# DeltaNet steps: keys and queries of a chunk side by side as one stationary operand

## The chip, the cores and the metric

The kernel runs on one core of one Trainium2 chip. The core has five engines that work at the same time: TensorE (PE) for matrix products, VectorE (DVE), ScalarE (ACT) and GpSimd (POOL) for the rest, SyncE (SP) for issuing transfers, and 16 DMA engines. Each engine runs its instructions in the order in which they were put in; semaphores make it wait for others. The metric is the time of one execution in microseconds (us), the median of several; smaller is better. A profile comes from one further execution.

## The reference

The program is a two-layer diffusion backbone over 256 latent and 256 context tokens of width 1024, in float32. Each layer is half a SwiGLU FFN, a token mixer, and half a FFN. The mixer of layer 0 is a bidirectional gated DeltaNet with 8 heads of width 128; that of layer 1 is windowed attention. The change is in the DeltaNet. Its tokens are cut into chunks of 64; within a chunk a triangular system is solved, and from chunk to chunk a 128x128 state is carried, once forwards and once backwards through the sequence:

```python
kb = k * beta[..., None]
lower = jnp.where(strict, jnp.einsum('nhcid,nhcjd->nhcij', kb, k) * decay, 0.0)
rhs = jnp.concatenate([v * beta[..., None], kb * jnp.exp(gc)[..., None]], axis=-1)
uw = lax.linalg.triangular_solve(lower, rhs, left_side=True, lower=True, unit_diagonal=True)
u, w = uw[..., :dv], uw[..., dv:]
qk = jnp.einsum('nhcid,nhcjd->nhcij', q, k) * decay
qg = q * jnp.exp(gc)[..., None]
kd = k * jnp.exp(g_last[..., None] - gc)[..., None]

def step(state, inp):
    u_c, w_c, qk_c, qg_c, kd_c, a_c = inp
    v_new = u_c - jnp.einsum('nhik,nhkv->nhiv', w_c, state)
    o = jnp.einsum('nhik,nhkv->nhiv', qg_c, state) + jnp.einsum('nhij,nhjv->nhiv', qk_c, v_new)
    state = state * a_c[..., None, None] + jnp.einsum('nhjk,nhjv->nhkv', kd_c, v_new)
    return state, o
```

In each step the state is multiplied by something made from the chunk's keys and by something made from its queries.

## The kernel before

The kernel keeps 128x512 tiles: 128 features by 512 tokens, or 128 tokens by four pieces of 128 features. The FFN and all projections are products of 128x128 weights with 128x512 activations; each float32 operand is split in a high and a low part, and three products of those make one accurate one (rows `mm<-u 128x512`). The DeltaNet's own small products (`mm<-u 128x128`, `64x128`, `64x64`) are plain float32, and the profile has two records for each of those.

**Order.** The kernel is written as tasks (Python generators) under a planner, `Sched`. The planner has a clock of its own, with a cost for each operation (a matmul's `ns`, a cost per element on the other engines). Whenever PE would have to wait for a task's operand by that clock, it steps other tasks. So the order of the instructions on all engines is fixed when the program is built, and an edit in one task moves the work of others. All matmuls are issued from one line, L280 (transposes on PE from L285), all other operations from L184; the tiles tell them apart.

**DeltaNet.** Units of projection come in the order `DN_ORDER`: keys, gate z, queries, values of heads 0 to 3 (group 0), then keys, values, queries, z of heads 4 to 7 (group 1). Each unit is convolved over the tokens (`u<-mm,cw,u`, five taps on DVE) and put through SiLU (`dn_unit`). Chunks are kept in four pairs q; a pair is a forward chunk on partitions 0 to 63 and its backward partner on 64 to 127. For each group runs `dn_group`: `dn_prep` makes the K·K products (`mm<-u 64x64`, `dn_pairs`) and their decay; `dn_solve` inverts the triangular blocks, 31 column steps of two DVE operations (`u<-big`, `big<-big,u`), then two transposes on DVE (`STREAM_TRANSPOSE big<-big`), then 32x32 products on PE (`mm<-big,ub`, `mm<-ub,u`); `dn_kq` makes the K·Q products and multiplies the decay on (`u<-mm,u` 128x512). There is one solve per group, solve 0 and solve 1. Group 1's keys, queries, values and decayed keys Ke pass through DRAM (`KTD`, `QD`, `VD`, `KD`), and are loaded when the chains of group 0 are done.

**Chains.** `dn_chain(h)` runs the eight steps (`STEPS`) of one head; four heads of a group run interleaved, chain 0 then chain 1. `dn_expand` puts the two 64x64 blocks of a pair into block-diagonal 128x128 tiles U and KQ. In each step with s≥1:

1. two matmuls with the 64 columns of a chunk's keys as stationary operand, one into each half of the partitions of `ps`, each with its direction's state S (a column pair, K);
2. DVE: r = neg·ps + Vt, one operation over 128 partitions (`u<-mm,neg,u`);
3. PE: U·r; ACT copies it as w;
4. PE: two products of a half of Ke (64 rows) with w (a Ke pair); two column-half products of the queries with S (a Q pair); KQ·w;
5. DVE: two updates of S (`u<-u,aS,mm`); ACT: a copy o and qs = eg·(Q·S) (`u<-mm,eg`); POOL adds them.

`dn_out` normalises the outputs by pairs of heads, transposes them and multiplies by the gate. The product of z with the output gain (`u<-u,ogain`) belongs to the z units, which are stored to `ZD`.

Of the kernel before, what the change touches and what calls it, by code (L numbers as in the profile page):

```python
# [213 lines left out]
class Kernel:  # L214
# [842 lines left out]
    def dn_gates(self, ps):  # L1057
# [52 lines left out]
        nc.vector.tensor_scalar(out=self.neg, in0=self.eg, scalar1=-1.0, scalar2=None, op0=ALU.mult)  # L1110
        self.kdw = self.const([128, 2, 4, 8], "kdw")
# [5 lines left out]
    def dn_unit(self, kind, h, ps):  # L1117
# [21 lines left out]
        yield self.at(acc)  # L1139
        for o, i in zip(self.pieces(t, True), self.pieces(acc, False)):  # L1140
            self.act(out=o, in_=i, func=AF.Silu)
        if kind < 2:
            (self.qT if kind == 0 else self.kT)[h] = t
        if kind == 0:
            sq = self.u()
            self.act(out=sq, in_=t, func=AF.Square)
            self.qsq[h] = sq
            return
# [25 lines left out]
    def dn_ss(self, sq, g, dst):  # L1174
# [12 lines left out]
        for i in range(4):  # L1187
            del sq[4 * g + i]

    def dn_pairs(self, ps, lhs, rhs, g, qp):  # L1190

        for q2 in range(2):
            for i in range(4):
                for half in range(2):
                    c0 = 128 * (2 * qp + q2) + 64 * half
                    o = 256 * q2 + 64 * i
                    self.mm(ps[64 * half:64 * half + 64, o:o + 64], lhs[4 * g + i][:, c0:c0 + 64],
                            rhs[4 * g + i][:, c0:c0 + 64], ns=75)

    def dn_prep(self, g):  # L1200
# [27 lines left out]
        for qp in range(2):  # L1228
            ps = self.mmt()
            self.dn_pairs(ps, self.kT, self.kT, g, qp)  # L1230
            G.append(self.u())
            self.act(out=G[qp], in_=ps, func=AF.Copy)
            yield 500
# [153 lines left out]
    def dn_expand(self, g, k):  # L1387
# [8 lines left out]
        for s, (q, e) in enumerate(self.STEPS):  # L1396
# [5 lines left out]
            else:  # L1402
                src = self.UB[g][:, x:x + 4, :]
            for hf in (slice(0, 64), slice(64, 128)):
                dst = tiles[s % nb].rearrange("p (h i) -> p h i", h=4)[hf, :, hf]
                if k and g == 0:
# [6 lines left out]
    def dn_chain(self, h):  # L1413
# [4 lines left out]
        while (h, 0) not in self.Ke or (h, 1) not in self.Ke:  # L1418
            yield 300
        kT, Vt = self.kT[h], self.Vt[h]  # L1420
        half = [slice(0, 64), slice(64, 128)]
        for s, (q, e) in enumerate(self.STEPS):
            cs = slice(128 * q, 128 * q + 128)
            c0 = [128 * q, 128 * q + 64]
            while (g, 0, s) not in self.blk:
# [42 lines left out]
            self.step[h] = s  # L1468
            yield self.at(po[:, 0:256])
            eg = self.eg[:, e, q, h:h + 1]  # L1470
            o = O[:, cs] if e == 0 else wv
            self.act(out=o, in_=po[:, 128:256], func=AF.Copy)
# [9 lines left out]
        self.chained.add(h)  # L1482
        for d in (self.kT, self.qT, self.Vt):
            del d[h]
# [10 lines left out]
    def dn_group(self, g):  # L1495
# [7 lines left out]
        if g:  # L1503
# [8 lines left out]
            for h in hs:  # L1512
                load(self.Ke, (h, 0), self.KD[2 * h - 8])
            for d, src in ((self.kT, self.KTD), (self.qT, self.QD)):
                for h in hs:
                    load(d, h, src[h - 4])
            for h in hs:
# [9 lines left out]
    def dn_out(self, p):  # L1527
# [29 lines left out]
        for h in hs:  # L1557
# [4 lines left out]
            t = self.u()  # L1562
            for o, i, z in zip(self.pieces(t, False), self.pieces(ps, True), self.pieces(zg[h], False)):
                nc.vector.tensor_tensor(out=o, in0=i, in1=z, op=ALU.mult)
            ps = None
# [27 lines left out]
    def deltanet(self, nxt):  # L1593
# [15 lines left out]
        self.KD = self.dp.tile([8, 128, 512], F32, name="KD", tag="KD")  # L1609
        self.QD = self.dp.tile([4, 128, 512], F32, name="QD", tag="QD")  # L1610
        self.KTD = self.dp.tile([4, 128, 512], F32, name="KTD", tag="KTD")
        self.VD = self.dp.tile([4, 128, 512], F32, name="VD", tag="VD")
# [291 lines left out]
```

## Time and profile before

| what | value |
|---|---|
| runs | 1927.81, 1928.87, 1933.45 us; median 1928.87 |
| profiled execution | 1928.68 us; its span 1926.9 us, granted PE clock 0.992 |
| first FFN | about 0 to 385 us |
| DeltaNet | about 385 to 800 us; solve 0 486.75 to 552.10, solve 1 606.65 to 685.70, chain 1 699.70 to 771.30 |
| two FFNs | about 800 to 1540 us |
| attention and last FFN | about 1540 to 1927 us |

How to read it: a row of the timeline or of the weight loads gives start, busy time, engine (PEld is a weight load), line, operation, the tiles (out<-in), the shape and a count of records; in brackets the idle time ahead and what ended it. A row of a table by window gives the window's length, then each engine's busy time with its count of instructions, the granted PE clock, the share of the DMA engines, and GB/s. In a row of instructions grouped by form the busy time and the mean in ns stand behind the bar, then the idle time ahead of them. The chain of waits follows the end of the program back from wait to wait. Matmul ends are modelled, and a few per cent of the records can be missing, so prices of matmuls are taken from starts.

### The profile page before, as it was taken

How to read it: one execution, taken by the hardware profiler on the slowest of the kernel's cores; microseconds unless marked ns; L12 is line 12 of the kernel's file. 1: busy time of each engine (PE TensorE's matmuls, PEld its weight loads, DVE VectorE, ACT ScalarE, POOL GpSimd, SP SyncE). 2: the span in 40 equal slices, each digit the busy share in tenths (PEclk: the TensorE clock that was granted, in tenths of full speed). 3: DMA queues.
4: the chain of work that ended last, by engine and by line, in shares of the span. 5: the costliest groups of instructions: out<-in, count | busy, mean ns of one | idle time of the engine just before them, and what ended most of it. 6: DMA issues, size and time to landing. Idle time of an engine off the chain costs nothing.

```text
span 1926.9 us, 30122 instructions
## 1 busy us (share of the span) xinstructions
PE 1868.2 (97%) x11335; PEld 1558.2 (81%) x11335; DVE 1278.8 (66%) x2097; ACT 949.4 (49%) x2062; POOL 649.3 (34%) x597
## 2 busy tenths in 40 slices
PE   7999999999999999999999999999999999899999
PEld 5878788887777766887888888888888899689999
DVE  4897878865986975478988655743333355956555
ACT  4545535457466555465455344641322248865442
POOL 3344434453545536254444124420000047230000
PEclk9999999999999999999999999999999999999999
DMA  9655554423222252444655454433223425125652
GB/s 292 209 199 202 177 186 170 141 61 115 83 68 87 66 182 83 162 156 150 208 196 195 170 190 155 153 126 109 89 90 106 132 66 110 45 67 176 197 176 88
DMA packets 242665, 271.31 MB, mean 141 GB/s; under 512 B 11047, under 2 KB 198719, under 8 KB 242519
## 3 DMA queue, kind: packets, MB, share of 16 engines
q1 hardware_dynamic: 242231, 269.21, 43.1%
q8 instruction: 89, 1.46, 0.3%
q14 instruction: 57, 0.47, 0.1%
q0 software_dynamic: 144, 0.11, 0.0%
q10 hardware_dynamic: 144, 0.07, 0.0%
HBM read 258.86 MB, written 10.49 MB: 140 GB/s over the span
## 4 chain that ended last, share of the span: by engine, by line
PE 55%; DVE 7%; ACT 3%; issue 3%; POOL 1%; DMA 1%; POOLq 0%; DVEq 0%; ACTq 0%; SPq 0%
PE mm L280 54%; DVE u L184 7%; ACT u L184 3%; PE mm L285 1%; POOL u L184 1%; DVE st L184 0%; DVE big L184 0%; DMA u<-ZD 0%; DMA u<-XD 0%; DVE ub L184 0%; ACT L184 0%; POOLq L184 0%; DVEq L184 0%; DVE sc L184 0%; ACT sc L184 0%
## 5 line engine op out<-in xcount | busy, mean ns | idle before, releaser
L280 PE MATMUL mm<-u 128*128 128x512 f32 (+5 forms) x10112 | 1784.9, 342 | 21.2 <-ACT u L184 8.2
L280 PEld LDWEIGHTS mm<-u 128*128 128x128 f32 (+2 forms) x10112 | 1490.4, 185 | 296.4 <-issue 42.0
L184 POOL TENSOR_TENSOR u<-u 128x512 f32<-128x512 f32 (+4 forms) x389 | 430.2, 1112 | 908.8 <-ACT u L184 868.9
L184 ACT ACTIVATE u<-u 128x512 fp32r<-128x512 f32 (+8 forms) x339 | 162.1, 490 | 494.0 <-DVE u L184 478.7
L184 ACT ACTIVATE u<-mm 128x128 f32<-128x128 f32 (+3 forms) x356 | 141.7, 413 | 262.4 <-PE mm L280 199.4
L184 DVE TENSOR_TENSOR u<-raw,u 128x512 fp32r<-128x512 f32 (+2 forms) x272 | 217.3, 842 | 27.7 <-ACT u L184 26.6
L184 DVE SCALAR_TENSOR_TENSOR u<-u,cc 128x512 f32<-128x512 f32 x196 | 228.2, 1164 | 4.5 <-DMA u<-in_ada_w 1.2
L184 DVE TENSOR_TENSOR u<-ub,u 128x512 fp32r<-128x512 f32 x254 | 200.3, 832 | 17.3 <-ACT u L184 15.9
L184 ACT ACTIVATE u<-raw 128x512 fp32r<-128x512 f32 (+1 forms) x374 | 205.9, 604 | 11.0 <-DMA raw<-in_ffn_w 6.6
L184 ACT ACTIVATE u<-u,cc 128x512 f32<-128x512 f32 x224 | 152.0, 711 | 83.2 <-DMA u<-in_ada_w 76.6
L184 DVE TENSOR_TENSOR u<-u,mm 128x512 f32<-128x512 f32 (+1 forms) x88 | 54.5, 620 | 206.5 <-PE mm L280 198.2
L184 POOL TENSOR_TENSOR u<-raw,u 128x512 fp32r<-128x512 f32 x98 | 130.3, 1354 | 140.2 <-ACT u L184 123.7
L184 ACT ACTIVATE u<-ub 128x512 fp32r<-128x512 f32 (+1 forms) x284 | 156.1, 605 | 9.5 <-PE mm L280 4.4
L184 DVE SCALAR_TENSOR_TENSOR u<-mm,mod,u 128x256 f32<-128x256 f32 x192 | 86.1, 477 | 108.6 <-PE mm L280 108.3
L184 DVE TENSOR_TENSOR u<-u 128x512 fp32r<-128x512 f32 (+5 forms) x125 | 84.4, 676 | 73.1 <-ACT u L184 71.6
L184 DVE SCALAR_TENSOR_TENSOR u<-u,mod 128x256 f32<-128x256 f32 (+1 forms) x140 | 89.1, 688 | 23.9 <-ACT u L184 23.6
L184 ACT ACTIVATE u<-u,mod 128x256 fp32r<-128x256 f32 (+1 forms) x124 | 56.2, 501 | 52.3 <-DVE u L184 51.6
L184 DVE SCALAR_TENSOR_TENSOR u<-mm,cw,u 128x510 f32<-128x510 f32 (+1 forms) x96 | 71.2, 743 | 8.1 <-ACT u L184 6.4
L285 PE MATMUL mm<-ident,u 128*128 128x128 f32 (+3 forms) x361 | 57.2, 291 | 15.3 <-DVE u L184 7.7
L285 PEld LDWEIGHTS mm<-ident,u 128*128 128x128 f32 (+3 forms) x361 | 43.9, 150 | 27.8 <-ACT u L184 7.5
L280 PE MATMUL mm<-u,ones 128*32 128x512 f32 (+2 forms) x172 | 38.8, 557 | 13.0 <-DVE u L184 8.9
L184 POOL TENSOR_TENSOR u<-ub,u 128x512 fp32r<-128x512 f32 x30 | 41.2, 1396 | 9.8 <-ACT u L184 9.5
(116 smaller groups left out, 567.2 us busy)
## 6 DMA issues: line engine op xcount, KB each, us to landing
u<-in_ada_w SPq DMA_DIRECT2D x256, 256.0 KB, 5.7
ub<-in_ffn_w SPq DMA_DIRECT2D x59, 1024.0 KB, 5.2
raw<-in_ffn_w SPq DMA_DIRECT2D x57, 1024.0 KB, 5.2
raw<-in_dn_w_in SPq DMA_DIRECT2D x16, 1024.0 KB, 5.7
ub<-in_ada_w SPq DMA_DIRECT2D x12, 512.0 KB, 7.3
ub<-in_ffn_w SPq DMA_DIRECT2D x8, 768.0 KB, 4.6
raw<-in_ffn_w SPq DMA_DIRECT2D x8, 768.0 KB, 4.5
raw<-in_dn_w_out SPq DMA_DIRECT2D x4, 1024.0 KB, 6.2
```

The lines of the kernel that those rows point to most:

```text
L184: r = f(*a, **k)
L280: self.nc.tensor.matmul(out, lhsT, rhs, start=start, stop=stop, **kw)
L285: self.nc.tensor.transpose(out, in_, self.ident[:k, :k])
```

## The change

Keys and queries of each chunk stand side by side in tiles AB, so that 128 columns of AB are the keys of one chunk and its queries. In AB[0] keys are the left half, in AB[1] the right; a forward and a backward tile per head.

- **Step.** Two full products AB·S give K·S and Q·S of both directions. The Q pair goes. Each product has K·S in one half of its partitions and Q·S in the other, so r takes two DVE operations of 64 partitions, and qs two ACT operations, which stand right behind U·r instead of behind the copy of o.
- **Exchanged chunks.** The query halves land on the other partitions, so outputs are kept with the two chunks of a pair exchanged: `dn_expand` writes KQ off the diagonal, `eg` and the squares of q are written with halves exchanged, `dn_out` takes three pieces in another order. `neg` gets its own exponential, since `eg` is exchanged now.
- **Transposes.** Heads 0 to 3 have no contiguous keys of a pair any more; their transposes become products of a column half with the identity, eight per head in place of four transposes.
- **DRAM.** `KTD` and `QD` become `AD`; group 1's keys and queries go out in 16 stores of 128x4x64 (256 bytes in a row) in place of 8 of 128x512, and come back in 8 loads of 128x512.

```diff
@@ dn_gates
-        self.act(out=fl(self.eg), in_=p3[:, 0:64], func=AF.Exp)
+        for i in range(2):
+            self.act(out=fl(self.eg)[64 * i:64 * i + 64], in_=p3[64 - 64 * i:128 - 64 * i, 0:64], func=AF.Exp)
...
@@ dn_unit
+        if kind < 2 and h < 4:
+            if kind == 1:
+                self.AB[h] = (t, self.u())
+            AB = [x.rearrange("p (s c x i) -> p s c x i", s=2, c=2, x=2) for x in self.AB[h]]
+            ac = acc.rearrange("p (s c t) -> p s c t", s=2, c=4)
+            for i in range(2):
+                self.act(out=AB[i][:, :, :, (1 - kind) ^ i, :], in_=ac[:, :, 2 * i:2 * i + 2, :], func=AF.Silu)
...
-            self.tr(ps[:, 128 * q:128 * q + 128], t[:, 128 * q:128 * q + 128])
+            if kind == 1 and h < 4:
+                for i in range(2):
+                    self.mm(ps[64 * i:64 * i + 64, 128 * q:128 * q + 128], self.part(1, h, q, i), self.ident, ns=135)
+            else:
+                self.tr(ps[:, 128 * q:128 * q + 128], t[:, 128 * q:128 * q + 128])
@@ dn_kq
-                nc.sync.dma_start(out=self.QD[i], in_=self.qT.pop(4 + i))
-                nc.sync.dma_start(out=self.KTD[i], in_=self.kT.pop(4 + i))
+                for kind, t in ((0, self.qT.pop(4 + i)), (1, self.kT.pop(4 + i))):
+                    tv = t.rearrange("p (q y i) -> p q y i", q=4, y=2)
+                    for y in range(2):
+                        dst = self.AD[i][:, y].rearrange("p (q x i) -> p q x i", q=4, x=2)[:, :, (1 - kind) ^ y, :]
+                        nc.sync.dma_start(out=dst, in_=tv[:, :, y, :])
@@ dn_chain
-                    self.mm(ps[half[i], 0:128], kT[:, c0[i]:c0[i] + 64], S[:, e ^ i, :], ns=135)
-                yield self.at(ps[:, 0:128])
-                nc.vector.scalar_tensor_tensor(out=r, in0=ps[:, 0:128], scalar=self.neg[:, e, q, h:h + 1], in1=Vt[:, cs],
-                                               op0=ALU.mult, op1=ALU.add)
+                    self.mm(sl[i], AB[i][:, c0[i]:c0[i] + 128], S[:, e ^ i, :])
+                yield self.at(*sl[0:2])
+                for i in range(2):
+                    nc.vector.scalar_tensor_tensor(out=r[half[i]], in0=sl[i][half[i]],
+                                                   scalar=self.neg[half[i], e, q, h:h + 1], in1=Vt[half[i], cs],
+                                                   op0=ALU.mult, op1=ALU.add)
...
-            self.mm(ps[:, 128:256], U, r)
+            self.mm(sl[2], U, r)
+            eg = self.eg[:, e, q, h:h + 1]
+            if s:
+                for i in range(2):
+                    o = half[1 - i]
+                    self.act(out=qs[o], in_=sl[i][o], func=AF.Copy, scale=eg[o])
...
-            if s:
-                for i in range(2):
-                    self.mm(po[half[i], 0:128], qT[:, c0[i]:c0[i] + 64], S[:, e ^ i, :], ns=135)
-            self.mm(po[:, 128:256], KQ, w)
+            self.mm(po[:, 0:128], KQ, w)
...
-                self.act(out=qs, in_=po[:, 0:128], func=AF.Copy, scale=eg)
```

The planner's clock counts a full product longer (214 ns) than a column half (135 ns), and the new tasks have other waits, so it also puts the work around the chains in another order. On PE, between solve 0's 32x32 products and group 1's 64x64 products (in `dn_prep`), stood before (`128x512` are projections and fillers, `128x128` full products of chain 0):

```order
L280 MATMUL mm<-u 128x512 x2
L280 MATMUL mm<-big,ub 32x32 x32
...
L285 MATMUL mm<-ident,u 128x128 x4
L280 MATMUL mm<-u 128x512 x10
L280 MATMUL mm<-u 128x128 x4
L280 MATMUL mm<-u 128x512 x6
L280 MATMUL mm<-u 128x128 x12
L280 MATMUL mm<-u 128x512 x5
L285 MATMUL mm<-ident,u 128x128 x4
L280 MATMUL mm<-u 64x64 x16
```

and now, from the last two rows above on:

```order
L280 MATMUL mm<-u 128x512 x5
L285 MATMUL mm<-ident,u 128x128 x4
L280 MATMUL mm<-u 128x512
L280 MATMUL mm<-u 128x128 x8
L280 MATMUL mm<-u 128x512 x4
...
L280 MATMUL mm<-u 128x128 x4
L280 MATMUL mm<-u 128x512 x5
L280 MATMUL mm<-u 128x128 x3
L280 MATMUL mm<-u 128x512 x3
L280 MATMUL mm<-u 128x128 x6
L280 MATMUL mm<-u 128x512 x5
L285 MATMUL mm<-ident,u 128x128 x4
L280 MATMUL mm<-u 64x64 x16
```

Between the two rows of four transposes stand now 22 products 128x512 and 24 of 128x128, a whole step of chain 0. In turn 54 products 128x512 ahead of solve 0's 32x32 products became 34. At the other end of solve 1 the products of chain 0 no longer stand beside the solve; on DVE its end was before:

```order
L184 SCALAR_TENSOR_TENSOR u<-mm,cw,u 128x2x254
L184 SCALAR_TENSOR_TENSOR u<-mm,neg,u 128x128
L184 TENSOR_TENSOR u<-big 128x31
L184 TENSOR_TENSOR big<-big,u 128x31
L184 STREAM_TRANSPOSE big<-big 128x32x32 x2
L184 SCALAR_TENSOR_TENSOR u<-mm,neg,u 128x128 x2
L184 TENSOR_SCALAR u<-u,ogain 128x512
L184 COPY ub<-big 32x16x32 x4
L184 TENSOR_TENSOR u<-mm,u 128x512 x4
```

and is now, with the product by the gain and the four of K·Q moved ahead into the solve:

```order
L184 TENSOR_SCALAR u<-u,ogain 128x512
L184 TENSOR_TENSOR u<-big 128x207
...
L184 TENSOR_TENSOR u<-mm,u 128x512 x2
L184 TENSOR_TENSOR big<-big,u 128x6x26
L184 TENSOR_TENSOR u<-mm,u 128x512 x2
...
L184 TENSOR_TENSOR u<-big 128x31
L184 TENSOR_TENSOR big<-big,u 128x31
L184 STREAM_TRANSPOSE big<-big 128x32x32 x2
L184 COPY ub<-big 32x16x32 x4
```

On SP the stores and loads of group 1 now read:

```order
L184 DMA ZD<-u 128x512
L184 DMA AD<-u 128x4x64 x16
L184 DMA u<-VD 128x512 x4
L184 DMA u<-KD 128x512 x4
L184 DMA u<-AD 128x512 x8
```

Before, the same place held eight stores `QD<-u`, `KTD<-u` in turn, the loads of `VD` and `KD`, and eight loads of `KTD` and `QD`; the store of `ZD` still stands ahead of them, and waits for the product by the gain.

More of the change, by code (lines that the diff above doesn't have):

```diff
@@ L1109, in dn_gates @@
         self.neg = self.const([128, 2, 4, 8], "neg")
-        nc.vector.tensor_scalar(out=self.neg, in0=self.eg, scalar1=-1.0, scalar2=None, op0=ALU.mult)
+        self.act(out=fl(self.neg), in_=p3[:, 0:64], func=AF.Exp)
+        nc.vector.tensor_scalar(out=self.neg, in0=self.neg, scalar1=-1.0, scalar2=None, op0=ALU.mult)
         self.kdw = self.const([128, 2, 4, 8], "kdw")
@@ L1139, in dn_unit @@
         yield self.at(acc)
[L1140 to L1143, printed above, removed]
+        if kind < 2 and h < 4:
[5 more added lines that the diff above has]
+                self.act(out=AB[i][:, :, :, (1 - kind) ^ i, :], in_=ac[:, :, 2 * i:2 * i + 2, :], func=AF.Silu)
+            t = self.AB[h][1]
+        else:
+            for o, i in zip(self.pieces(t, True), self.pieces(acc, False)):
+                self.act(out=o, in_=i, func=AF.Silu)
+            if kind < 2:
+                (self.qT if kind == 0 else self.kT)[h] = t
         if kind == 0:
             sq = self.u()
-            self.act(out=sq, in_=t, func=AF.Square)
+            if h < 4:
+                sv = sq.rearrange("p (s c y i) -> p s c y i", s=2, c=2, y=2)
+                self.act(out=sv[:, :, :, 1, :], in_=AB[0][:, :, :, 1, :], func=AF.Square)
+                for c in range(2):
+                    self.act(out=sv[:, :, 1 - c, 0, :], in_=AB[1][:, :, c, 0, :], func=AF.Square)
+            else:
+                sv, tv = [x.rearrange("p (q y i) -> p q y i", q=4, y=2) for x in (sq, t)]
+                for y in range(2):
+                    self.act(out=sv[:, :, 1 - y, :], in_=tv[:, :, y, :], func=AF.Square)
             self.qsq[h] = sq
@@ L1188, in dn_ss, with part @@
             del sq[4 * g + i]
+    def part(self, kind, h, q, half):
+        if h >= 4:
+            return (self.kT if kind else self.qT)[h][:, 128 * q + 64 * half:128 * q + 64 * half + 64]
+        c = 128 * (q ^ half) + 64 * ((1 - kind) ^ half)
+        return self.AB[h][half][:, c:c + 64]
     def dn_pairs(self, ps, lhs, rhs, g, qp):
@@ L1194, in dn_pairs @@
                 for half in range(2):
[L1195 removed]
+                    q = 2 * qp + q2
                     o = 256 * q2 + 64 * i
[L1197 to L1198 removed]
+                    self.mm(ps[64 * half:64 * half + 64, o:o + 64], self.part(lhs, 4 * g + i, q, half),
+                            self.part(rhs, 4 * g + i, q, half), ns=75)
     def dn_prep(self, g):
@@ L1403, in dn_expand @@
                 src = self.UB[g][:, x:x + 4, :]
-            for hf in (slice(0, 64), slice(64, 128)):
-                dst = tiles[s % nb].rearrange("p (h i) -> p h i", h=4)[hf, :, hf]
+            halves = (slice(0, 64), slice(64, 128))
+            for y, hf in enumerate(halves):
+                dst = tiles[s % nb].rearrange("p (h i) -> p h i", h=4)[hf, :, halves[y ^ k]]
                 if k and g == 0:
@@ L1430, in dn_chain @@
             r, w, qs, wv = [tmp[:, 128 * i:128 * i + 128] for i in range(4)]
+            sl = [ps[:, 128 * i:128 * i + 128] for i in range(4)]
             yield self.at(S, U)
@@ L1482, in dn_chain @@
         self.chained.add(h)
-        for d in (self.kT, self.qT, self.Vt):
+        for d in (self.AB, self.Vt):
             del d[h]
@@ L1513, in dn_group @@
                 load(self.Ke, (h, 0), self.KD[2 * h - 8])
-            for d, src in ((self.kT, self.KTD), (self.qT, self.QD)):
-                for h in hs:
-                    load(d, h, src[h - 4])
+            for h in hs:
+                ab = {}
+                for y in range(2):
+                    load(ab, y, self.AD[h - 4][:, y])
+                self.AB[h] = (ab[0], ab[1])
             for h in hs:
@@ L1562, in dn_out @@
             t = self.u()
-            for o, i, z in zip(self.pieces(t, False), self.pieces(ps, True), self.pieces(zg[h], False)):
-                nc.vector.tensor_tensor(out=o, in0=i, in1=z, op=ALU.mult)
+            tv, pv, zv = [x.rearrange("p (s c t) -> p s c t", s=2, c=4) for x in (t, ps, zg[h])]
+            for o, i in ((slice(0, 2), slice(1, 4, 2)), (slice(2, 3), slice(2, 3)), (slice(3, 4), slice(0, 1))):
+                nc.vector.tensor_tensor(out=tv[:, :, o, :], in0=pv[:, :, i, :], in1=zv[:, :, o, :], op=ALU.mult)
+            pv = None
             ps = None
```

27 lines of the change are left out of this document (14 added, 13 removed).

## The prediction

> **What bounds the kernel now.** I read the page from its top: busy shares, the chain of work that ended last, the DMA queues.
>
> ```profile
> PE 1868.2 (97%) x11335; PEld 1558.2 (81%) x11335; DVE 1278.8 (66%) x2097; ACT 949.4 (49%) x2062; POOL 649.3 (34%) x597
> ...
> q1 hardware_dynamic: 242231, 269.21, 43.1%
> ...
> PE 55%; DVE 7%; ACT 3%; issue 3%; POOL 1%; DMA 1%; POOLq 0%; DVEq 0%; ACTq 0%; SPq 0%
> ```
>
> Over the whole span PE is the bound. The change touches only the DeltaNet, so I cut that stretch at its hand-overs: first solve starts; its last DVE operation ends; group 1's first 64x64 products; second solve starts; its last transpose ends; chain 1 starts; chain 1 ends.
>
> ```profile
> core 0: us, PE busy (x) PEld busy (x) DVE busy (x) ACT busy (x) POOL busy (x), PEclk, DMA share, GB/s
> ...
> 486.75:552.10 65.35, 62.07 (x329) 48.84 (x328) 62.20 (x106) 33.05 (x71) 34.96 (x29) 0.97 0.29 85
> 552.10:579.58 27.48, 24.91 (x367) 18.70 (x366) 20.05 (x34) 20.15 (x66) 11.55 (x15) 1.00 0.22 56
> 579.58:606.65 27.07, 27.07 (x235) 19.64 (x234) 16.81 (x40) 18.23 (x50) 14.66 (x20) 1.00 0.17 63
> 606.65:685.70 79.05, 76.77 (x486) 54.44 (x484) 70.20 (x149) 47.95 (x151) 41.65 (x60) 1.00 0.26 81
> 685.70:699.70 14.00, 11.75 (x352) 9.88 (x353) 9.95 (x21) 9.36 (x29) 5.75 (x10) 0.88 0.88 304
> 699.70:771.30 71.60, 68.82 (x515) 48.53 (x514) 43.15 (x122) 36.85 (x127) 36.71 (x62) 1.00 0.30 104
> ```
>
> In the two solves (first and fourth row) DVE is busy 62.20 of 65.35 and 70.20 of 79.05 us: a solve is a row of DVE operations, and what PE does beside it is filler whose amount the planner picks. Between the solves (second and third row) and in chain 1 (last) PE is the full engine. So the DeltaNet is a relay: solve 0 on DVE, PE up to the 64x64 products and on to the second solve, solve 1 on DVE, chain 1 on PE. PE work saved counts only in PE's legs, and work that the new order moves into one costs there. The chain of waits shows the hand-over after the second solve:
>
> ```profile
> 681.73 3.97 DVE big L184 x2
> ...
> 687.07 5.10 PE mm L280 x191
> 692.16 1.58 issue
> 694.83 51.08 PE mm L280 x409
> ```
>
> **Prices on PE.** Weight loads show when matmuls start; a float32 product has two records.
>
> ```profile
> 641.95 0.20 PEld L280 LDWEIGHTS mm<-u 128*64 128x64 f32 x4 [0.24 <-issue]
> 642.32 0.85 PEld L280 LDWEIGHTS mm<-u 128*128 128x128 f32 x7 [0.17 <-issue]
> ...
> 647.37 0.62 PEld L280 LDWEIGHTS mm<-u 64*128 64x128 f32 x8 [0.36 <-ACT u L184]
> 648.16 1.04 PEld L280 LDWEIGHTS mm<-u 128*128 128x128 f32 x10 [0.17 <-issue]
> ...
> 653.22 0.85 PEld L280 LDWEIGHTS mm<-u 128*64 128x64 f32 x16 [0.35 <-issue]
> 654.24 0.76 PEld L280 LDWEIGHTS mm<-u 128*128 128x128 f32 x4 [0.17 <-issue]
> ```
>
> One column pair alone takes 642.32−641.95 = 0.37 us, four in a run 1.02/4 = 0.255 each: the two halves run side by side. The eight records at 647.37 are a Ke pair and a Q pair, 0.79, so a Ke pair is 0.42. Gone: 56 Q pairs, 56×0.37 = −20.7. The K pair turns into two full products. The trace has no such two alone; the Ke pair is the nearest row, since it too loads 128 columns for each of its two products, so 0.42 against 0.37: +0.05 a step, +2.8. From above two products at the run price of 0.255 bound it, 0.51: +0.14, +7.8. From below, 0.37−0.255 = 0.115 is what a lone switch into column halves costs, which full products don't have: −0.07, −3.6. The Trainium skill, "TensorE: Matmul & The Clock Gate", "LDWEIGHTS (loading the stationary operand)", has a load's time go by its columns alone, columns over 1.2 in ns; that speaks against the change. An estimate from that page: four loads of 64 columns 0.21 us, four of 128 0.43, so +0.21 a step, and leg 5 below would be −4.5 and the sum 1935. The 0.42 agrees with the second figure, but the 0.255 to 0.37 of the pair here don't with the first, and the rows decide. K transposes of heads 0 to 3 become eight column-half products a head for four transposes: 4×(1.02−0.53), the transposes from the second and third last row here:
>
> ```profile
> 555.65 4.24 PE L280 MATMUL mm<-u 128*128 128x512 f32 x18
> 559.98 0.85 PE L285 MATMUL mm<-ident,u 128*128 128x128 f32 x4
> ...
> 561.22 0.75 PE L280 MATMUL mm<-big,ub 32*32 32x32 f32 x64
> ...
> 579.05 0.60 PE L285 MATMUL mm<-ident,u 128*128 128x128 f32 x4
> 579.58 2.61 PE L280 MATMUL mm<-u 128*64 128x64 f32 x68
> ```
>
> That is +2.0. In all PE loses 20.7−2.8−2.0 = 16 us of work. How much of it reaches the end?
>
> **Leg 1, PE from solve 0 to the 64x64 products.** In the new order 20 fewer 128x512 products stand ahead of the first solve's 32x32 products. DVE releases those (561.22), so this wins nothing. Behind them, ahead of the 64x64 products at 579.58, stand 22 more 128x512 products and one step of chain 0's four heads. A 128x512 product takes (559.98−555.65)/18 = 0.24: 5.3. The step, four each of state pairs and Ke pairs at 0.42 and eight full products at 0.21: 5.0. Sum 10.3; PE idles 27.48−24.91 = 2.6 there and may fill that. Taken +10, ends +8 and +10.3.
>
> **Leg 2, to the second solve.** DVE is busy 16.81 of 27.07 us in it.
>
> ```profile
> 583.58 1.12 DVE L184 SCALAR_TENSOR_TENSOR u<-mm,neg,u 128x128 f32<-128x128 f32 x4
> ...
> 599.21 0.74 DVE L184 SCALAR_TENSOR_TENSOR u<-mm,cw,u 128x510 f32<-128x510 f32 x1
> ...
> 605.10 1.64 DVE L184 SCALAR_TENSOR_TENSOR u<-u,aS,mm 128x128 f32<-128x128 f32 x6
> ```
>
> By the new order eight more half r operations (an r over 64 partitions has the same 128 columns, so I price it as a whole one, 1.12/4 = 0.28: +2.2) and four more convolution taps (+3.0) stand in it, and six state updates fewer (−1.6). Content +3.5, of a DVE that has 10 us idle: taken +1.5, ends 0 and +3.5.
>
> **Leg 3, solve 1.** 14 more half r (+3.9), four fewer taps (−3.0), two fewer updates (−0.5); from the stretch behind the solve come forward the o_gain product (0.45) and group 1's four K·Q mask products (2.48). Content +3.3. Against it the waits that DVE has here:
>
> ```profile
> DVE u L184 <- ACT u L184: 3.5, 2, 2.3
> DVE u L184 <- PE mm L280: 3.2, 6, 1.0
> ```
>
> 6.7 us, of which part goes, since the solve's last third has only its own operations left. Taken +1.5, ends −3.4 (all waits gone) and +3.3.
>
> **Leg 4, behind the solve.** The two pieces that came forward stood behind it (the first row is one of the solve's own, from its last third):
>
> ```profile
> 666.99 0.36 DVE L184 TENSOR_TENSOR u<-big 128x207 f32<-128x207 f32 x1
> ...
> 686.02 0.45 DVE L184 TENSOR_SCALAR u<-u,ogain 128x512 f32<-128x512 f32 x1
> 686.40 3.37 DVE L184 COPY ub<-big 32x512 f32<-32x512 f32 x4
> 689.80 2.48 DVE L184 TENSOR_TENSOR u<-mm,u 128x512 f32<-128x512 f32 x4
> ```
>
> −2.9. In the new order nothing of chain 0 is left beside them, so PE has a hole ahead of the second solve's 32x32 products, some 15 us as long as DVE's last third of the solve. The granted clock falls after such stops: 0.88 in the row 685.70:699.70, 1.7 us lost of 14. A longer hole costs little more: +0.5, ends 0 and +1.7 (the same loss again).
>
> **Leg 5, chain 1.** PE is busy 68.82 of 71.60. 28 steps lose a Q pair (−10.4) and pay the dearer state products (+1.4): −9.0, ends −12.4 and −6.5. Behind it the order is as before.
>
> **Costed at nothing.** ACT gains 56 half qs, one more per step:
>
> ```profile
> L184 ACT ACTIVATE u<-mm,eg 128x128 f32<-128x128 f32 x56 | 20.4, 364 | 0.1
> ```
>
> 0.36 us each, on an engine busy 47.95 of 79.05 and 36.85 of 71.60. They stand ahead of the copy of w, but wait only for the state products and run while DVE makes r and PE U·r; without that cover a step is 0.4 later, with three other heads to fill it. The exchanged gate operations and the one extra dn_out product per head are under 1 us, beside PE. The transfers: 16 stores with 256-byte rows replace 8 of 128x512 on SP.
>
> ```profile
> 686.50 0.34 SPq L184 DMA_DIRECT2D ZD<-u  x1
> 686.89 0.42 SPq L184 DMA_DIRECT2D QD<-u  x1
> ...
> 692.81 1.82 SPq L184 DMA_DIRECT2D u<-VD  x4
> ```
>
> The 8 took 692.81−686.89 = 5.9 us, and chain 1's loads are queued behind them. The 16 still follow the o_gain product, but this now stands ahead of the solve's operation at 666.99, not behind the end of the transposes at 685.70; of the 18.7 us between, eight state updates and four taps of before fall out (8×0.27+4×0.74 = 5.1). So they start some 14 us earlier against the solve's end and have 14+5.9 = 20 us. By bytes they take 5.9 again; from above, the mean packet of q1, 0.431×16×1926.9/242231 = 0.055 us, times 8192 rows over 16 engines is 28. I take the bytes, hidden.
>
> **Sum.** Leg 1 +10, leg 2 +1.5, leg 3 +1.5, leg 4 −2.9 and +0.5, leg 5 −9.0: +1.6. Against the profiled execution (1928.68; span 1926.9 and 1.8 around it; the median of the runs, 1928.87, is 0.2 above) 1930.3, so 1930.
>
> **Rivals.** *Faster, the relay shortens.* Chain 0 runs ahead, so solve 1 loses its waits: leg 1 +8, leg 2 0, leg 3 −3.4, the rest as above: −6.8, 1922; in the limit where DVE's legs adapt and PE's whole saving counts, 1913. For it speaks PE at 97%; against it that 20 more filler products are free for DVE's legs, not for PE's. *Slower, DVE keeps its extra halves.* Every extra r is on DVE's path: leg 2 +3.5, leg 3 +3.3, and in chain 1 the r of four heads queue as at 583.58, 2.2 instead of 1.12 us a step, of which half shows over seven steps, +3.9: +9.3, 1938. The forecast has 3 of these 10.7 us; it decides once about 7 show; against it stands DVE's 43.15 of 71.60 in chain 1. *Slower, stores.* Near 28 us they delay chain 1 by 28−20 = 8: 1938. The Trainium skill, "DMA: Bandwidth & Descriptors", "Specifications", gives 512 bytes as the least transfer for full rate, with a read-modify-write below it, which speaks for this rival; no row here has such a store alone.
>
> **How the numbers follow.** Forecast 0.40, faster rival 0.32, DVE rival 0.20, stores 0.08. A change under 0.3% (5.8 us) can't be told from none in this kernel, so faster 0.32, same 0.40, slower 0.28. The forecast's own range is 1924 to 1934. The range reaches to the faster limit's near side, 1914, and past the slower cases by the upper price of the state products in chain 1 (−6.5 for −9.0), 1941.
>
> **What would show it.**
>
> ```profile
> L280 PE MATMUL mm<-u 128*64 128x128 f32 x704 | 62.0, 287 | 0.0
> ```
>
> Right: these column-half records fall to 320 (448 of the steps go, 64 of transposes come); DVE has 112 half r of about 0.28; the first 64x64 products of group 1 come near 590, the second solve's last transpose near 698, chain 1's first U near 710, its length near 63 us; a hole on PE ahead of the second solve's 32x32 products. Wrong: a half r well under 0.28 or a state pair away from 0.42; a chain 1 that stays near 71 us, with DVE or ACT waits in it; the solve longer than 81 us; loads of VD that land after the solve's end.

## The result, and the profile after

The changed kernel takes 1960.12 us (median; 1956.39 to 1961.38) against 1928.59: ratio 1.0154, 95% interval 1.0143 to 1.0166. It is 31 us slower; 1930 was forecast, with 1914 to 1941 as the range. First the page of the changed kernel, busy shares and the chain that ended last:

```profile
PE 1869.6 (95%) x11159; PEld 1570.9 (80%) x11159; DVE 1309.1 (67%) x2161; ACT 968.4 (49%) x2130; POOL 650.3 (33%) x597
...
PE 73%; DVE 15%; ACT 6%; issue 4%; POOL 1%; DMA 1%; SPq 0%; DVEq 0%; ACTq 0%; POOLq 0%
```

PE is as busy as before in a span 32 us longer, though 176 of its records are gone; DVE's share of the chain rose from 7% to 15%. The change did what it says: column-half records of 128x128 fell from 704 to 256 and 64, and r is 112 half operations.

```profile
L184 ACT ACTIVATE u<-mm,eg 64x128 f32<-64x128 f32 x112 | 40.6, 362 | 22.3 <-PE mm L280 19.6 <-POOL u L184 1.1
L184 DVE SCALAR_TENSOR_TENSOR u<-mm,neg,u 64x128 f32<-64x128 f32 x112 | 39.1, 349 | 10.9 <-PE mm L280 8.7
L280 PE MATMUL mm<-u 128*64 128x128 f32 x256 | 18.1, 279 | 0.0
L280 PE MATMUL mm<-ident,u 128*64 128x128 f32 x64 | 4.7, 280 | 1.7 <-ACT u L184 1.7
```

The same hand-overs as in the prediction cut the stretch; here chain 1 runs from its first r on DVE to its last. The table by window of the changed kernel:

```profile
core 0: us, PE busy (x) PEld busy (x) DVE busy (x) ACT busy (x) POOL busy (x), PEclk, DMA share, GB/s
482.98:550.77 67.79, 63.03 (x329) 49.11 (x327) 64.49 (x103) 32.27 (x75) 35.86 (x30) 0.97 0.32 89
550.77:594.15 43.38, 38.50 (x440) 30.10 (x441) 29.27 (x54) 28.29 (x91) 14.03 (x18) 0.92 0.19 53
594.15:626.58 32.43, 29.73 (x210) 22.37 (x209) 23.23 (x47) 24.69 (x70) 22.17 (x29) 1.00 0.27 88
626.58:713.56 86.98, 70.47 (x434) 54.94 (x434) 75.60 (x161) 52.19 (x163) 41.10 (x58) 0.91 0.34 94
713.56:734.93 21.37, 15.96 (x313) 13.04 (x314) 10.45 (x29) 6.76 (x18) 2.38 (x6) 0.65 0.62 225
734.93:805.45 70.52, 63.94 (x390) 50.83 (x389) 49.81 (x141) 44.22 (x149) 34.66 (x56) 0.90 0.20 65
```

and of the kernel before, for the last two rows in the same cut:

```profile
685.70:706.10 20.40, 18.15 (x397) 14.41 (x399) 15.27 (x37) 11.42 (x37) 8.14 (x16) 0.92 0.93 329
706.10:772.90 66.80, 64.02 (x483) 44.81 (x480) 38.67 (x109) 35.19 (x121) 34.60 (x56) 1.00 0.23 76
```

From solve 0's last transposes (552.10, now 550.77) to the 64x64 products: 27.48 to 43.38, +15.9. To the second solve: 27.07 to 32.43, +5.4. Solve 1: 79.05 to 86.98, +7.9. To chain 1's first r: +1.0. Chain 1: 66.80 to 70.52, +3.7. The end of solve 0 comes 1.3 earlier, and from the last r to the next FFN (its first 128x256 product, at 801.7 and now at 832.7) it takes 1.6 less. Together the 31 us. Every leg of the relay got longer, also chain 1, which was to win 9 us; and in three of the legs (the way to the 64x64 products, solve 1, chain 1) the granted clock stands at 0.90 to 0.92 where it was 1.00.

### The profile page after: what moved, and what is told of

It is laid out like the page before. It is cut to its first block, busy times and chain, and to the rows that moved or that the text cites. A ratio compares the mean times of both kernels' runs of the same rounds, so it can differ in the third digit from the quotient of the medians.

```text
span 1958.9 us, 29875 instructions
## 1 busy us (share of the span) xinstructions
PE 1869.6 (95%) x11159; PEld 1570.9 (80%) x11159; DVE 1309.1 (67%) x2161; ACT 968.4 (49%) x2130; POOL 650.3 (33%) x597
## 4 chain that ended last, share of the span: by engine, by line
PE 73%; DVE 15%; ACT 6%; issue 4%; POOL 1%; DMA 1%; SPq 0%; DVEq 0%; ACTq 0%; POOLq 0%
PE mm L280 71%; DVE u L184 12%; ACT u L184 5%; DVE big L184 2%; PE mm L285 2%; POOL u L184 1%; ACT L184 0%; DMA u<-in_x 0%; DMA u<-ZD 0%; DVE st L184 0%; DMA u<-XD 0%; DVE ub L184 0%; ACT ub L184 0%; ACT big L184 0%; DVE gs L184 0%
## 5 line engine op out<-in xcount | busy, mean ns | idle before, releaser
L280 PE MATMUL mm<-u 128*128 128x512 f32 (+4 forms) x9888 | 1780.5, 344 | 30.7 <-ACT u L184 14.3
L184 POOL TENSOR_TENSOR u<-u 128x512 f32<-128x512 f32 (+5 forms) x389 | 431.4, 1115 | 906.3 <-ACT u L184 868.4
L184 ACT ACTIVATE u<-u 128x256 f32<-128x256 f32 (+8 forms) x351 | 162.6, 479 | 491.5 <-DVE u L184 478.3
L184 ACT ACTIVATE u<-u,cc 128x512 f32<-128x512 f32 x224 | 152.0, 711 | 83.0 <-DMA u<-in_ada_w 77.7
L184 DVE TENSOR_TENSOR u<-u 128x512 fp32r<-128x512 f32 (+5 forms) x125 | 84.3, 675 | 73.3 <-ACT u L184 71.6
L184 DVE SCALAR_TENSOR_TENSOR u<-u,mod 128x256 f32<-128x256 f32 (+1 forms) x140 | 89.0, 687 | 23.9 <-ACT u L184 23.6
L184 DVE SCALAR_TENSOR_TENSOR u<-mm,cw,u 128x510 f32<-128x510 f32 (+1 forms) x96 | 71.4, 744 | 9.3 <-ACT u L184 7.2
L184 ACT ACTIVATE u<-mm,eg 64x128 f32<-64x128 f32 x112 | 40.6, 362 | 22.3 <-PE mm L280 19.6
```

Source lines behind the costliest of these rows:

```text
L184: r = f(*a, **k)
L280: self.nc.tensor.matmul(out, lhsT, rhs, start=start, stop=stop, **kw)
```

## The experiments

The theory after the result: **order** (a projection unit and a step of chain 0 moved between solve 0 and the 64x64 products) or **half operations** (r twice on DVE, qs twice on ACT); rivals: the clock, and the layout with its stores. All stages below are from one profiled execution each, which can lie some 6 us off the median; columns: from the end of solve 0's last transposes to the second solve's start (the rows above start at the beginning of those transposes), solve 1, from there to chain 1's first r, first to last r. Each ratio is to runs of the kernel before that were taken together with that kernel's. Each edit also lets the planner set the order anew around it.

| kernel | median us | ratio (95%) to the kernel before | to solve 1 | solve 1 | to r | chain 1 |
|---|---|---|---|---|---|---|
| before | 1928.59 | 1 | 50.3 | 79.0 | 20.4 | 66.8 |
| changed | 1960.12 | 1.0154 (1.0143–1.0166) | 71.6 | 87.0 | 21.4 | 70.5 |
| e1_order_back | 1954.79 | 1.0126 (1.0100–1.0153) | 51.0 | 97.3 | 21.7 | 70.5 |
| e2_order_only | 1942.04 | 1.0061 (1.0040–1.0082) | 72.0 | 73.9 | 18.6 | 69.2 |
| e3_qs_late | 1971.21 | 1.0213 (1.0186–1.0240) | 73.2 | 94.2 | 20.5 | 73.6 |
| e4_step_undone | 1956.27 | 1.0148 (1.0100–1.0195) | 75.0 | 73.9 | 19.1 | 76.9 |
| e5_one_r | 1940.44 | 1.0064 (1.0049–1.0079) | 48.4 | 84.6 | 23.2 | 70.4 |
| e6_one_qs | 1950.62 | 1.0117 (1.0102–1.0132) | 52.7 | 96.4 | 21.2 | 66.8 |
| e7_one_both | 1937.84 | 1.0050 (1.0035–1.0065) | 48.7 | 78.3 | 31.7 | 62.6 |
| e8_warm | 1971.19 | 1.0227 (1.0210–1.0244) | 51.4 | 93.4 | 32.8 | 77.4 |
| e9_zd_act | 1935.47 | 1.0028 (1.0015–1.0041) | 49.1 | 77.7 | 23.9 | 62.9 |
| e10_half_r | 1955.79 | 1.0146 (1.0132–1.0160) | 53.7 | 101.2 | 19.1 | 74.2 |
| e11_half_stores | 1939.66 | 1.0065 (1.0052–1.0078) | 50.1 | 79.0 | 28.7 | 73.5 |
| e12_k_products | 1934.60 | 1.0035 (1.0023–1.0048) | 49.5 | 79.1 | 21.2 | 69.1 |
| e13_r_off_dve | 1941.05 | 1.0054 (1.0041–1.0067) | 46.8 | 68.5 | 49.6 | 66.8 |
| e14_after_r_off | 1949.70 | 1.0097 (1.0082–1.0113) | 50.0 | 71.4 | 45.8 | 70.3 |
| e15_after_r_off2 | 1958.18 | 1.0145 (1.0132–1.0159) | 69.5 | 75.3 | 34.1 | 69.8 |

**Order.** e1_order_back is the changed kernel with one planner number altered:

```diff
-  self.mm(ps[64 * i:64 * i + 64, 128 * q:128 * q + 128], self.part(1, h, q, i), self.ident, ns=135)
+  self.mm(ps[64 * i:64 * i + 64, 128 * q:128 * q + 128], self.part(1, h, q, i), self.ident, ns=53.5)
```

> The changed kernel with one number of the planner altered: it counts each column-half product of the K transposes as 53.5 ns in place of 135, as much as half a transpose before. All operations stay. With it the 207, 135 and 28 products 128x512 stand again between the landmarks (mask products of group 0, solve 0, group 1's 64x64 products), as in the kernel before. If the order caused the loss: 1925 to 1935, with group 1's 64x64 products back near 580 us. If the half operations of the step on DVE and ACT caused it: 1950 to 1960, second solve still some 8 us longer than before, chain 1 still 70 us.

1954.79: the way to solve 1 is 51.0 us again, but solve 1 has grown to 97.3. Of the 20 us 10 come back in the solve, which now holds one step of chain 0 more (40 half r for 32); the median falls by 5. That is the time expected of the half operations, with the second solve longer than expected (18 us for 8). So the order mainly chose where the loss falls.

e2_order_only gives the kernel before the changed kernel's order, with `self.s.tick(163)` behind each K transpose of heads 0 to 3.

> The kernel before with one number of the planner altered: it counts a K transpose of heads 0 to 3 as 270 ns in place of 107. All operations stay as before; around solve 0 the products 128x512 now stand 205, 114 and 54 instead of 207, 135 and 28, near the 205, 114 and 51 of the changed kernel, with a whole step of chain 0 ahead of group 1's 64x64 products. If the order caused the loss: 1950 to 1960. If the half operations did: 1928 to 1938 (the first PE leg's +10 less what the later legs win).

1942.04: +21.6 on the way to solve 1, −5.1 in it. Neither expectation was met: order alone costs 13 us, less than half of the loss.

**The step.** e3_qs_late moves the two qs behind the copy of o.

> The changed kernel with the two ACT operations qs moved back behind the copy of o, where the one qs stood before, so that they no longer stand ahead of the copy of w. If that queue on ACT lengthens the step (0.36 us twice per head and step, 56 steps): 10 to 20 us less than the changed kernel, 1940 to 1950. If the order caused the loss: within 4 us of the changed kernel's 1960.

1971.21, 11 us more, and both expectations failed. In solve 1 PE's waits for ACT rise from 4.6 to 13.1 us; why, the runs don't settle.

e4_step_undone takes K·S and Q·S as four column-half products out of AB, with one r and one qs.

> The changed kernel with its step undone: two column-half products for K and two for Q out of the AB tiles, one r over 128 partitions, one qs behind the copy of o. The layout, the exchanged halves, the K transposes and the AD stores of the changed kernel stay, and so does its order around solve 0 (205, 114 and 54 products 128x512). If the step's half operations caused the loss: 1930 to 1938. If the order did: 1950 to 1960, like the kernel before in this order. If stores or layout do something besides: it differs from that kernel.

1956.27. Solve 1 is 73.9, exactly as in e2_order_only, whose step and order it shares: the step's share in solve 1 is gone. But it is 14 us above that kernel, in the way to solve 1 and in chain 1 (76.9 against 69.2), so layout and stores do cost something. And it is only 4 us below the changed kernel (its own runs go from 1952.6 to 1966): in that order, what the half operations cost and what the saving on PE brings nearly cancel. The next kernels have the restored order of e1_order_back; those with one r or one qs leave out the values of one half, and serve for their time alone. e5_one_r:

```diff
-  for i in range(2):
-      nc.vector.scalar_tensor_tensor(out=r[half[i]], in0=sl[i][half[i]], ...
+  nc.vector.scalar_tensor_tensor(out=r, in0=sl[0], scalar=self.neg[:, e, q, h:h + 1], in1=Vt[:, cs], ...
```

> The changed kernel with the restored order (the planner's 53.5 ns, measured 1955), and r as one DVE operation over all 128 partitions of the first product; this leaves out the right values of one half of r. It has 56 DVE operations fewer; all else stays. If the doubled r on DVE stretches solve 1 and chain 1: some 10 us less than 1955, with solve 1 near 90 us instead of 97 and the chain shorter. If qs on ACT or the clock does: within 4 us of 1955.

1940.44, 14 us less than e1_order_back, 12.6 of it in solve 1: the doubled r is the larger part of that kernel's 26. Chain 1 is as long as before (70.4). e6_one_qs has `self.act(out=qs, in_=sl[1], func=AF.Copy, scale=eg)` for the two ACT operations.

> The changed kernel with the restored order (1955), and qs as one ACT operation over 128 partitions of the second product, still ahead of the copy of w; this leaves out the right values of one half of qs. If the queue on ACT ahead of w lengthens the step: 5 to 15 us less than 1955. If the doubled r does: within 4 us of it.

4.2 us less, 3.7 of it in chain 1. e7_one_both has both edits.

> Both: one r and one qs, restored order; the values of one half of each are left out. The step has then no half operations and two matmuls less than the kernel before. If the half operations are the whole loss: 1915 to 1930, the saving on PE shows. If the clock, the layout or the stores hold a part: 1932 to 1945.

1937.84. Solve 1 (78.3) is as before the change and chain 1 shorter than ever, 62.6, so the saving on PE exists: 4.2 of the 9 us. But chain 1's first r comes 31.7 us after the solve. Its SP queue and its chain of waits say why:

```profile
691.46 0.34 SPq L184 DMA_DIRECT2D ZD<-u  x1
691.85 10.87 SPq L184 DMA_DIRECT2D AD<-u  x16
702.83 1.92 SPq L184 DMA_DIRECT2D u<-VD  x4
```

```profile
703.89 4.46 DMA u<-VD
...
708.39 12.50 PE mm L280 x55
```

Here the store of z waits for a product that the planner put behind the solve, the 16 stores stand behind it, and the loads of V behind those. e9_zd_act issues the z stores with `nc.scalar.dma_start`:

> The kernel with one r and one qs (values of one half of each left out, measured 1938, with 31.7 us from the end of solve 1 to chain 1's first r, against 20.4 before), and the stores of z issued by ACT instead of SP, so that the 16 AD stores on SP do not stand behind the store that waits for the gain product. If that queue makes the 11 us: the gap falls to 20 to 23 us and the time to 1925 to 1930. If the gap has another cause (cold PE, instruction fetch): gap 28 us or more, 1934 to 1940.

The gap falls to 23.9; the median, 1935.47, by less than was expected of the queue. With no half operation left, and loads of V issued 6.3 us behind the solve (7.1 in the kernel before), this kernel still does not beat the kernel before (ratio 1.0028, 1.0015 to 1.0041).

**The clock.** e8_warm adds PE work that nobody reads:

```diff
+  if g and j >= 20:
+      m = min(128, r * n)
+      jk = self.mmt()
+      for _ in range(2):
+          self.mm(jk[:, 0:m], self.ident, tmp[:, 0:m], ns=0.0)
...
+  if g:
+      for i in range(2):
+          self.mm(sl[2], AB[i][:, c0[i]:c0[i] + 128], S[:, e ^ i, :], ns=0.0)
```

> The changed kernel with the restored order (1955) and extra work for PE whose results nobody reads: behind each of the last 11 column steps of solve 1 two products 128x128 of the identity with that step's result, and in each step of chain 1 the two state products a second time (28 steps, 0.4 us each, 11 us of work), counted as nothing by the planner. If low granted clock after idle PE is what costs: clock near 1.0 in the stretch of the second solve's end and in chain 1, and 3 to 10 us less than 1955 in spite of the work. If the clock is only a sign of waiting: 0 to 12 us more.

Its windows: second part of solve 1, the gap, chain 1.

```profile
660.00:703.00 43.00, 36.51 (x227) 29.20 (x227) 33.63 (x74) 24.45 (x81) 16.25 (x28) 0.88 0.10 34
703.00:735.80 32.80, 23.56 (x364) 17.82 (x360) 13.51 (x34) 9.93 (x23) 4.87 (x8) 0.74 0.79 231
735.80:813.20 77.40, 71.49 (x489) 59.85 (x489) 46.66 (x137) 40.91 (x145) 30.24 (x55) 0.93 0.16 53
```

1971.19, 16 us more, which neither expectation had: chain 1 takes 6.9 us more and the clock rises only from 0.90 to 0.93; the gap grew with the z store behind the solve, as in e7_one_both. Filling PE does not pay here. Since this work never brought the clock back to 1.00, this run can't say what the clock costs by itself; other kernels can, at the end of this section.

**Single parts, put on the kernel before.** e10_half_r:

```diff
-  nc.vector.scalar_tensor_tensor(out=r, in0=ps[:, 0:128], scalar=self.neg[:, e, q, h:h + 1], in1=Vt[:, cs], ...
+  for i in range(2):
+      nc.vector.scalar_tensor_tensor(out=r[half[i]], in0=ps[half[i], 0:128],
+                                     scalar=self.neg[half[i], e, q, h:h + 1], in1=Vt[half[i], cs], ...
```

> The kernel before with one part of the change alone: r in two DVE operations of 64 partitions each. The order around solve 0 stays as before (207, 135 and 28 products 128x512). If the doubled r carries the loss: solve 1 longer by 5 to 13 us, chain 1 by 0 to 4, 1934 to 1945. If it needs the rest of the change to hurt: within 4 us of 1929.

1955.79, +27 us, beyond both expectations. Solve 1 has 101.2 us and chain 1 74.2 (in a profiled execution 5 us above the median). First its windows of solve 1 and chain 1, then the r in solve 1 as one group:

```profile
610.70:711.90 101.20, 88.26 (x574) 63.55 (x572) 84.10 (x174) 54.87 (x166) 45.91 (x66) 0.90 0.32 100
731.00:805.20 74.20, 71.07 (x491) 47.24 (x487) 46.93 (x133) 31.96 (x123) 31.61 (x58) 0.88 0.16 54
```

```profile
L184 DVE SCALAR_TENSOR_TENSOR u<-mm,neg,u 64x128 f32<-64x128 f32 x40 | 13.9, 348 | 6.6 <-PE mm L280 6.0
```

(in the kernel before)

```profile
L184 DVE SCALAR_TENSOR_TENSOR u<-mm,neg,u 128x128 f32<-128x128 f32 x19 | 6.2, 338 | 0.8 <-PE mm L280 0.8
```

(and DVE's waits in e10_half_r again)

```profile
DVE u L184 <- PE mm L280: 9.1, 9, 3.1
DVE u L184 <- ACT u L184: 3.4, 3, 2.3
DVE big L184 <- ACT big L184: 1.9, 1, 1.9
```

DVE is busy 84.10 for 70.20, 13.9 more, and idle 17.1 for 8.85, 8.3 more. The r explain 7.7 of the busy time (13.9 for 40 halves; 6.2 for 19 whole ones before); 2.6 is the K·Q products that the planner moved forward into the solve, and the remaining 3.6 is spread over the other operations. How much of the 8.3 is the halves' own waits, and how much the lower clock (0.90 for 1.00) or the new order inside the solve, is not separated. The one edit makes nearly the whole loss by itself, in the kernel's old order around solve 0.

e11_half_stores puts each of the 8 stores out in two transfers of 128x4x64.

> The kernel before with keys and queries of group 1 stored in 16 transfers of 128x4x64 in place of 8 of 128x512; order unchanged on PE. If 256-byte rows or the number of transfers matter where the stores are not covered (they took 5.9 us here, right ahead of chain 1's loads): 3 to 6 us more, 1932 to 1935. If only bytes count: within 1 us of 1929.

```profile
687.45 0.34 SPq L184 DMA_DIRECT2D ZD<-u  x1
687.84 1.35 SPq L184 DMA_DIRECT2D QD<-u  x2
...
699.77 1.34 SPq L184 DMA_DIRECT2D KTD<-u  x2
701.21 2.02 SPq L184 DMA_DIRECT2D u<-VD  x4
```

The stores take 701.21−687.84 = 13.4 us for the same bytes as 5.9 before, and the gap is 8.3 us longer. The median is 10 us longer; the profiled execution, 6 us above its median, also has chain 1 at 73.5 for 66.8, and that is the clock, as shown below. In e12_k_products the four transposes of a head are eight column-half products.

> The kernel before with the K transposes of heads 0 to 3 as eight column-half products each, order unchanged on PE. By prices of the trace +2 us of PE work ahead of solve 0, and it stands on the path to it: 1929 to 1932. If these products are the source of what the layout costs (14 us between the step undone and the order alone): 1936 or more.

Ratio 1.0035 (1.0023 to 1.0048), 4 to 9 us. The profiled execution lies 5 us below the median and has no more than 2.3 us of it, in chain 1, not ahead of solve 0; so where it comes from is not settled.

**r off DVE.** Open was whether DVE's time counts, or the delay of r for PE. In e13_r_off_dve, on the kernel before, ACT and POOL make r in chain 0; e14_after_r_off and e15_after_r_off2 do the same to the changed kernel in the restored and in its own order.

```diff
+  if g:
       nc.vector.scalar_tensor_tensor(out=r, ...)
+  else:
+      self.act(out=r, in_=ps[:, 0:128], func=AF.Copy, scale=self.neg[:, e, q, h:h + 1])
+      yield self.at(r)
+      nc.gpsimd.tensor_tensor(out=r, in0=r, in1=Vt[:, cs], op=ALU.add)
```

> The kernel before with r of chain 0 taken off DVE: ACT multiplies K·S by neg, POOL adds Vt; chain 1 as before, order around solve 0 as before. If DVE's own time in solve 1 sets its length: solve 1 shorter by up to the 6.4 us that its 19 r take there, 1922 to 1927. If the wait for r inside a step sets it (two engines and a hand-over more, 0.5 to 1 us a step and head): solve 1 as long or longer, 1929 to 1940.

> The changed kernel with the restored order (1955) and r of chain 0 taken off DVE: ACT makes its two halves, POOL adds Vt in one operation. Chain 1 keeps the two half r on DVE. If DVE's own time in solve 1 is the loss: solve 1 falls from 97 to 80 us or less and the time to 1935 to 1942. If the latency of the step is: 1950 or more.

> The changed kernel in its own order (1960) with r of chain 0 taken off DVE in the same way. Solve 1 has 32 half r, 11.2 us. If DVE's time there is what counts: solve 1 falls from 87 to 77 us or less, and what is left over the kernel before (about 20 us) is the order's first leg and the chain: 1948 to 1953. If the latency does: 1956 or more.

Solve 1 falls to 68.5, 71.4 and 75.3, from 79.0, 97.3 and 87.0: DVE's queue sets the solve's length. Not all of that is r, for in e13_r_off_dve the solve also holds 24 state updates for 34 and 25 convolution taps for 28. The solves fell as the first expectations had it, the times (1941.05, 1949.70, 1958.18) did not. None is a gain over the kernel before, since the gap grows to 34 to 50 us. Chain 1 starts only when chain 0 is done and its loads have come; in e13_r_off_dve the chain of waits ends so:

```profile
697.40 3.42 DMA u<-KD
...
701.59 20.43 PE mm L280 x113
```

The last qs of chain 0 starts there at 710.2, and chain 1's first r at 719.7; in the kernel before at 695.5 and 706.1. This suggests that in the kernel before two paths, the solve on DVE and chain 0, released chain 1 about together, and that each edit here made one shorter and the other longer.

**The clock by itself.** The kernel before, e2_order_only, e11_half_stores, e12_k_products and e13_r_off_dve have the same operations in chain 1, on PE, DVE and ACT in the same order. PE is idle 2.5 to 2.8 us in each. The clock is 1.00, 0.95, 0.89, 0.95 and 1.00, and chain 1 takes 66.8, 69.2, 73.5, 69.1 and 66.8 us. First chain 1 in e13_r_off_dve and in e11_half_stores, with the first 8 us of the latter:

```profile
719.70:786.50 66.80, 64.02 (x483) 44.81 (x480) 38.64 (x109) 35.09 (x121) 34.52 (x56) 1.00 0.19 62
```

```profile
715.30:788.85 73.55, 71.00 (x484) 49.71 (x484) 39.06 (x109) 35.35 (x121) 34.52 (x56) 0.89 0.20 64
715.30:723.30 8.00, 8.00 (x51) 5.68 (x50) 2.79 (x8) 1.97 (x8) 0.46 (x1) 0.66 0.20 75
```

then the 8 us with PE's longest stop and the 8 us behind them, in the kernel before and in e11_half_stores, both 40 us behind the first r:

```profile
746.10:754.10 8.00, 6.37 (x59) 4.42 (x59) 4.72 (x15) 6.01 (x20) 2.08 (x5) 1.00 0.72 233
754.10:762.10 8.00, 7.83 (x73) 5.72 (x68) 7.65 (x19) 3.86 (x13) 6.48 (x9) 1.00 0.19 65
```

```profile
755.30:763.30 8.00, 6.37 (x50) 4.35 (x49) 4.39 (x14) 5.31 (x17) 0.46 (x1) 0.90 0.39 123
763.30:771.30 8.00, 8.00 (x44) 5.89 (x44) 4.88 (x16) 3.12 (x14) 4.29 (x8) 0.50 0.51 175
```

The stops are alike, and the clock falls behind one and not behind the other. So the clock is a cause of its own: with the same work and the same idle time it makes chain 1 up to 6.7 us longer. The 7.4 us of chain 1 in e10_half_r (0.88, PE idle 3.1) go with it too. In the changed kernel, e1_order_back, e14_after_r_off and e15_after_r_off2, whose chain 1 has the changed step, it was 0.90 each time. Why it falls behind one stop and not behind another, the runs don't show.

The parts tested alone, order 13, half r 27, half stores 10 and K products 6 us, add up to more than the whole loss, so they are not shares of it.

## Why the prediction was wrong

- **Bound and relay**: right. The legs, cut at the same hand-overs, add up to the loss.
- **Leg 1, +10**: the work was right, the term too small. Measured +15.9: PE busy 38.50 for 24.91, +13.6, of which the clock of 0.92 makes up to 3.5 (0.08×43.38), so some 10 of work; and 2.3 more idle. I had let idle PE fill up, to +8 at best; instead waits and clock came on top.
- **Leg 2, +1.5**: +5.4. PE, full before, is idle 2.7 of 32.43 and busy 2.7 longer, and DVE does 23.23 for 16.81.
- **Leg 3, +1.5**: this step failed. I set DVE's waits, as something that would shrink, against the added operations; but a half r waits for PE itself, and the solve's operations stand behind it in DVE's queue. In solve 1:

```profile
L184 DVE SCALAR_TENSOR_TENSOR u<-mm,neg,u 64x128 f32<-64x128 f32 x32 | 11.2, 349 | 4.2 <-PE mm L280 3.6
```

```profile
DVE u L184 <- PE mm L280: 7.6, 5, 3.3
DVE u L184 <- ACT u L184: 0.6, 1, 0.6
```

The waits rose (idle 11.4 for 8.85) and the busy time rose by 5.4, so solve 1 is 7.9 longer, although it holds the r of 16 steps of a head for 19 before (13 half r more, not 14); my bound, all of the content on the path, was +3.3. In the old order around solve 0 the changed step costs 18 us there (e1_order_back), the edit to two r alone 22 (e10_half_r). The price was low too: four heads' r take 2.95 us a step, 0.37 each, not 0.28.

```profile
598.15 2.95 DVE L184 SCALAR_TENSOR_TENSOR u<-mm,neg,u 64x128 f32<-64x128 f32 x8
```

- **Leg 4, −2.9 and +0.5**: +1.0. The two pieces did come forward, and the hole on PE ahead of the 32x32 products came. The clock, 0.65 in 713.56:734.93 for 0.92 before, and 3.2 us more idle on PE go against the gain.
- **Leg 5, −9.0**: +3.7, by size the largest miss. It put waits and clock in chain 1 at nothing. PE's busy time stayed at 64 us under a clock of 0.90, so the work itself fell by up to 7 us (0.10×70.52) and the clock took it back. The rest is waits: PE idles 6.6 us for 2.8, its waits of over 0.5 us being these:

```profile
PE mm L280 <- ACT u L184: 3.9, 5, 1.0
PE mm L280 <- DVE u L184: 2.2, 3, 1.7
```

  With one r and one qs 4.2 us of the 9 appear (e7_one_both), under a clock of 0.93.
- **State pair at 0.42**: near. In a run of full float32 products of chain 1 with nothing between, 18 loads took 2.08 us; without the last load's own 0.19 that is 17 steps of 0.11, so 0.45 a pair of four records. The Trainium skill, "TensorE: Matmul & The Clock Gate", "LDWEIGHTS (loading the stationary operand)", gave an estimate of 0.43 by its rule: this agrees to 0.02.

```profile
733.48 2.08 PEld L280 LDWEIGHTS mm<-u 128*128 128x128 f32 x18
```

- **qs costed at nothing**: two for one cost 4 us, nearly all in chain 1 (e6_one_qs). In the changed kernel two heads' qs stand ahead of the first copy of w, and the chain of waits passes through them, as here in a step of chain 0 behind solve 0. The place alone is not the loss, for e3_qs_late, which moves them back, is slower:

```profile
585.65 0.36 ACT u L184
586.02 0.36 ACT u L184
586.39 0.36 ACT u L184
586.77 0.53 ACT u L184 x2
```

- **Stores hidden**: right for this kernel, by its order alone. They took 10.2 us, between the 5.9 and the 28 of the bounds, but began 13 us ahead of the solve's end (700.22). Uncovered, as in e7_one_both and e11_half_stores, the gap behind the solve was 8 to 11 us longer. The Trainium skill, "DMA: Bandwidth & Descriptors", "Specifications", puts the least transfer for full rate at 512 bytes; 13.4 for 5.9 us agrees, but the rows went from 512 elements (2 KB) to 64 (256 bytes) and the transfers doubled at once, so the runs don't say which of the two it is.

```profile
700.22 10.11 SPq L184 DMA_DIRECT2D AD<-u  x16
710.42 1.92 SPq L184 DMA_DIRECT2D u<-VD  x4
```

- **Rivals**: the loss is the DVE rival's mechanism, given 0.20 and 1938. It was too small since it counted content alone, and the order's leg 1 at work alone; and no rival had a lower clock in solve 1 and chain 1.
- **Signs of being wrong**: two showed, a solve longer than 81 us (87.0) and a chain 1 no shorter, with DVE and ACT waits in it.
- **A slip in reading**: the 0.53 of the transposes lies between the last two rows of that view, not the second and third last; the number is right.

## What to carry to other kernels

Splitting an operation by partitions halves no time: price each half as a whole one, and count what queues behind it on its engine, above all where another task's long row of operations shares that queue. A saving on the busiest engine is worth only what remains after the waits that the saving creates; test it with the cheap part undone (here one r in place of two) before building the layout for it. Where a planner sets the order, vary one of its numbers on the old kernel: that prices the move of work apart from the change. And before a few microseconds are put down to an edit, compare the granted clock of the two stretches.

## What the runs showed of the hardware

- A DVE operation over 64 partitions takes as long as one over 128: 349 ns for 64x128, 338 to 342 for 128x128; in a row, eight took 2.95 us (0.37 each) and four of 128 partitions 1.12 (0.28 each). On ACT likewise, 362 against 364 ns.
- The granted PE clock was not in proportion to PE's stops: with 2.5 to 2.8 us idle and the same operations chain 1 had 1.00, 0.95 or 0.89, and took 66.8, 69.1 to 69.2 or 73.5 us. In the gap ahead of it, 0.65 stood beside 5.4 us idle of 21.4.
